# A decoder trunk with split fp32 weights: the low part of every fourth weight unit by an accumulating DMA

## The chip, the cores and the metric

The kernel runs on one core of one Trainium2 chip. The metric is device time in microseconds of one execution. Five engines work side by side, each with its own queue in program order: TensorE (PE, matmul; PEld is its weight load), VectorE (DVE), ScalarE (ACT), GpSimd (POOL) and SyncE (SP, which here only issues DMAs). They wait for each other by semaphores.

## The reference

Two layers of a hybrid decoder at 256 tokens and width 1024, all in float32. Each layer is a SwiGLU feed-forward block, a mixer and another feed-forward block, each behind an RMSNorm; the first layer's mixer is latent attention beside a gated MLP over chunks, the second's a short gated convolution.

```
def swiglu(h, w_gate, w_up, w_down):
    return (jax.nn.silu(h @ w_gate) * (h @ w_up)) @ w_down

for layer in range(DEPTH):
    x = x + 0.5 * swiglu(rms_norm(x, ffn_pre_norm[layer]), ...)
    h = rms_norm(x, mix_norm[layer])
    x = x + (mla_sgu_mixer if layer % 2 == 0 else short_conv_mixer)(h, ...)
    x = x + 0.5 * swiglu(rms_norm(x, ffn_post_norm[layer]), ...)
return rms_norm(x, final_norm)
```

With 256 tokens every weight is used once, so about 170 MB of weights pass through the core in one execution.

## The kernel before

TensorE multiplies in a rounded 32-bit format (fp32r). To stay near float32 each operand is split in two: a rounded part, hi, and what rounding lost, lo = x - hi. A product is then three matmuls: hi by hi, hi by lo and lo by hi (`mm_b`, L315 to L317: activation hi by weight hi, activation hi by weight lo, activation lo by weight hi; L316 is the one that reads the weight's low part).

The weights come in 162 units, numbered from 0, of mostly 128 x 2048 numbers (1 MB), in the order of the list `plan`: 22 units of gate and up weights and 11 of the down projection for each of the four feed-forward blocks (f0 to f3), 10 units and 4 of output projection for the attention mixer between f0 and f1, 12 and 4 for the convolution between f2 and f3. Each unit goes through four steps in `prefetch`: SP issues a load from HBM into `raw` (L136); ScalarE writes `whi`, the rounded copy, in two pieces of 1024 columns (L139, 320 of them); VectorE writes `wlo` = raw - whi in the same two pieces (L140); TensorE uses both in 24 matmuls of 512 columns (other counts in the mixers). Units 0 and 1 are cut differently (L130, L131).

`raw`, `whi` and `wlo` have three buffers each. `weights()` is called when a unit is about to be used and prefetches three units ahead (LOOKAHEAD), so what holds a unit back is its buffers: whi and wlo of unit n are those of unit n-3, and raw of unit n is free again when unit n-3 has been converted. In an output projection (`project_out`) the last two units (TAIL) are used together, column block by column block, so their buffers come back only at its end.

The order of instructions on each engine is set by a scheduler at build time, from the order of the program and priorities. Beside the units, ScalarE and VectorE work off the gate of the pair of units before (`gate`: SiLU L368, product L369, copies L376 and L377 of the transposed result, which TensorE makes in L374), and the norms (L269, L280, L281, L346). POOL does little: some constants, a mask (L520) and four copies in the attention mixer (L634).

Of the kernel before, what the change touches and what calls it, by code (L numbers as in the profile page):

```python
# [19 lines left out]
F32 = mybir.dt.float32  # L20
# [3 lines left out]
AF = mybir.ActivationFunctionType  # L24
ALU = mybir.AluOpType
# [41 lines left out]
def trunk(ctx: ExitStack, tc: tile.TileContext, io: dict, out: bass.AP, stop=None):  # L67
    nc = tc.nc
    V, A, G, PE = nc.vector, nc.scalar, nc.gpsimd, nc.tensor
# [39 lines left out]
    def prefetch(upto):  # L109
        while len(ready) < min(upto, len(plan)):  # L110
            src = plan[len(ready)]
            w = math.prod(src.shape[1:])
            raw = rawp.tile([P, WMAX], F32, name="raw")
            hi = hip.tile([P, WMAX], F32R, name="whi")
            lo = lop.tile([P, WMAX], F32R, name="wlo")
            n = len(ready)
            if n < 2:

                rv, hv, lv = (t.rearrange("p (f n) -> p f n", f=2) for t in (raw, hi, lo))
                cuts = ((0, 1), (1, 2), (2, 4)) if n == 0 else ((0, 2), (2, 4))  # L120
                for k0, k1 in cuts:
                    e = slice(k0 * 256, k1 * 256)
                    k, c, m = 4 * n + k0, 2 * n + k0 // 2, k0 % 2
                    nc.sync.dma_start(xt[c][:, m:m + k1 - k0, :], io["xT"][:, k:4 * n + k1, :])
                    nc.sync.dma_start(rv[:, :, e], src[:, :, e])
                for k0, k1 in cuts:
                    for k in range(4 * n + k0, 4 * n + k1):
                        split_to(mv[k], xt[k // 2][:, k % 2, :], col(C_PRE0 + k))
                    e = slice(k0 * 256, k1 * 256)
                    A.activation(hv[:, :, e], rv[:, :, e], AF.Copy)  # L130
                    V.tensor_tensor(lv[:, :, e], rv[:, :, e], hv[:, :, e].bitcast(F32), ALU.subtract)  # L131
            else:
                dst = raw[:, :w]
                if len(src.shape) == 3:
                    dst = dst.rearrange("p (a n) -> p a n", a=src.shape[1])
                nc.sync.dma_start(dst, src)  # L136
                for q in range(0, w, STEP):
                    e = slice(q, min(q + STEP, w))
                    A.activation(hi[:, e], raw[:, e], AF.Copy)  # L139
                    V.tensor_tensor(lo[:, e], raw[:, e], hi[:, e].bitcast(F32), ALU.subtract)  # L140
            ready.append((hi, lo))

    used = [0]
# [1 line left out]
    def weights():  # L145
        prefetch(used[0] + 1 + LOOKAHEAD)
        w = ready[used[0]]
        used[0] += 1
        return w
# [19 lines left out]
    def col(c):  # L169
        return small[:, c:c + 1]  # L170
# [17 lines left out]
    def split_to(m, src, scale=None):  # L188

        if scale is None:  # L190
            return (A.activation(m[:, :T], src, AF.Copy),
                    V.tensor_tensor(m[:, T:], src, m[:, :T].bitcast(F32), ALU.subtract))
        return (A.activation(m[:, :T], src, AF.Copy, scale=scale),
                V.scalar_tensor_tensor(m[:, T:], src, scale, m[:, :T].bitcast(F32), ALU.mult, ALU.subtract))
# [205 lines left out]

    norm = Norm(C_PRE0)
    prefetch(2)
    for b in range(2):
        for h in range(2):
# [28 lines left out]
    for j in range(KD):  # L433
        if j % 2 == 0:
            hi, lo = weights()
# [5 lines left out]
        hi, lo = weights()  # L441
# [29 lines left out]
    for h in range(2):  # L471
        for b in range(2):
            e = slice(b * 512, (b + 1) * 512)
# [333 lines left out]
```

## Time and profile before

| | |
|---|---|
| median of 2 timed runs | 962.16 us (961.34 to 962.99) |
| the profiled execution | 962.89 us, of which the profile's span is 961.2 us |
| busy: PE, DVE, ACT, POOL | 98%, 59%, 51%, 1% of the span |
| HBM read | 171.62 MB, 180 GB/s over the span |
| granted TensorE clock | 0.996 of full speed, mean |

The span is from the first to the last instruction; the execution's own time has 1.7 us around it. Busy matmul time is modelled from a pipeline, so consecutive matmuls overlap in the rows; an idle time on TensorE shows as a gap with the name of what ended it. The chain that ended last is followed back from the last instruction; what is off that chain had time to spare.

### The profile page before, as it was taken

What the parts mean: (1) busy time and instruction counts of PE and PEld (TensorE: products, weight loads), DVE (VectorE), ACT (ScalarE), POOL (GpSimd) and SP (SyncE); (2) the same over time, 40 slices, a digit from 0 to 9 for tenths busy, and PEclk for the clock granted to TensorE, in tenths of its full rate; (3) what the DMA queues carried; (4) which work ended last, traced back from release to release, by engine and by line L of the source; (5) the groups of instructions that cost most, each with busy time, mean ns of one, the idle gap of its engine ahead of it and who ended that gap; (6) DMA issues with size and microseconds to landing.
All of it is one profiled execution on the core that took longest, in us unless ns stands there. A gap on an engine that the chain in (4) does not pass through costs nothing.

```text
span 961.2 us, 11528 instructions
## 1 busy us (share of the span) xinstructions
PE 942.2 (98%) x4588; PEld 785.1 (82%) x4588; DVE 564.3 (59%) x800; ACT 486.4 (51%) x736; POOL 5.3 (1%) x13
## 2 busy tenths in 40 slices
PE   7999999999999999999999999999999999999996
PEld 5888888898978888888888888888888888888885
DVE  5765554477767555554475555544898765555433
ACT  7454444384757444443374444434655554454432
POOL 0000000001000000000000000000000000000000
PEclk9999999999999999999999999999999999999998
DMA  7865556545514655565556555564446465555541
GB/s 265 269 210 183 176 185 197 186 154 175 175 58 162 217 177 178 193 197 178 187 178 203 177 177 186 186 197 175 176 176 203 148 218 177 190 198 180 175 132 44
DMA packets 57446, 173.42 MB, mean 180 GB/s; under 512 B 2992, under 2 KB 3888, under 8 KB 54832
## 3 DMA queue, kind: packets, MB, share of 16 engines
q1 hardware_dynamic: 57392, 172.68, 53.1%
q8 instruction: 36, 0.59, 0.2%
q14 instruction: 18, 0.15, 0.0%
HBM read 171.62 MB, written 1.05 MB: 180 GB/s over the span
## 4 chain that ended last, share of the span: by engine, by line
PE 96%; DVE 1%; ACT 1%; DMA 1%; SPq 0%; issue 0%; DVEq 0%; ACTq 0%
PE ps L317 27%; PE ps L315 27%; PE ps L316 26%; PE ps L179 5%; PE ps L180 2%; PE psb L374 2%; PE ps L184 1%; PE ps L185 1%; PE ps L186 1%; PE psb L275 1%; DMA raw<-in_f_gu 1%; PE ps L587 0%; PE ps L589 0%; PE ps L588 0%; PE ps L655 0%; DVE wlo L140 0%
## 5 line engine op out<-in xcount | busy, mean ns | idle before, releaser
L140 DVE TENSOR_TENSOR wlo<-raw,whi 128x1024 fp32r<-128x1024 f32 x320 | 378.5, 1220 | 305.1 <-ACT whi L139 305.1
L139 ACT ACTIVATE whi<-raw 128x1024 fp32r<-128x1024 f32 x320 | 321.8, 1050 | 322.4 <-issue 167.4
L315 PE MATMUL ps<-whi,mv 128*128 128x512 f32 x704 | 279.2, 397 | 6.3 <-ACT whi L130 6.3
L316 PE MATMUL ps<-wlo,mv 128*128 128x512 f32 x704 | 275.6, 391 | 0.8 <-DVE wlo L131 0.8
L317 PE MATMUL ps<-whi,mv 128*128 128x512 f32 x704 | 275.4, 391 | 0.0
L315 PE MATMUL ps<-whi,a 128*128 128x512 f32 x416 | 163.4, 393 | 0.0
L316 PE MATMUL ps<-wlo,a 128*128 128x512 f32 x416 | 162.8, 391 | 0.0
L317 PE MATMUL ps<-whi,a 128*128 128x512 f32 x416 | 162.6, 391 | 0.0
L315 PEld LDWEIGHTS ps<-whi,mv 128*128 128x128 f32 x704 | 132.8, 189 | 33.4 <-ACT whi L130 7.2
L316 PEld LDWEIGHTS ps<-wlo,mv 128*128 128x128 f32 x704 | 132.9, 189 | 28.2 <-DVE wlo L131 2.0
L317 PEld LDWEIGHTS ps<-whi,mv 128*128 128x128 f32 x704 | 132.7, 188 | 28.0
L317 PEld LDWEIGHTS ps<-whi,a 128*128 128x128 f32 x416 | 78.1, 188 | 16.1 <-issue 0.2
L316 PEld LDWEIGHTS ps<-wlo,a 128*128 128x128 f32 x416 | 78.3, 188 | 15.6
L315 PEld LDWEIGHTS ps<-whi,a 128*128 128x128 f32 x416 | 78.1, 188 | 15.6
L368 ACT ACTIVATE silu<-ps,rn 128x256 f32<-128x256 f32 x88 | 41.3, 469 | 70.6 <-DVE silu L369 70.6
L179 PE MATMUL ps<-mv,whi 128*128 128x512 f32 x192 | 67.0, 395 | 0.0
L369 DVE SCALAR_TENSOR_TENSOR silu<-ps,rn,silu 128x256 f32<-128x256 f32 x88 | 42.2, 480 | 22.2 <-ACT silu L368 22.2
L180 PE MATMUL ps<-mv,wlo 128*128 128x256 f32 x192 | 53.1, 279 | 0.0
L179 PEld LDWEIGHTS ps<-mv,whi 128*128 128x128 f32 x192 | 35.9, 188 | 7.9
L281 DVE SCALAR_TENSOR_TENSOR mv<-psb,small,mv 128x128 fp32r<-128x128 f32 x80 | 26.6, 347 | 19.3 <-ACT mv L280 19.3
L180 PEld LDWEIGHTS ps<-mv,wlo 128*128 128x128 f32 x192 | 36.1, 188 | 0.6 <-DVE wlo L140 0.4
L377 DVE TENSOR_TENSOR a<-psb,a 128x512 fp32r<-128x512 f32 x44 | 30.2, 685 | 5.4 <-ACT a L376 5.4
(183 smaller groups left out, 584.2 us busy)
## 6 DMA issues: line engine op xcount, KB each, us to landing
raw<-in_f_gu SPq DMA_DIRECT2D x86, 1024.0 KB, 5.2
raw<-in_f_dn SPq DMA_DIRECT2D x44, 1024.0 KB, 5.2
raw<-in_c_cz SPq DMA_DIRECT2D x8, 1024.0 KB, 5.0
raw<-in_e_in SPq DMA_DIRECT2D x7, 1024.0 KB, 4.8
raw<-in_e_out SPq DMA_DIRECT2D x4, 1024.0 KB, 5.1
raw<-in_c_b SPq DMA_DIRECT2D x4, 1024.0 KB, 4.8
raw<-in_c_out SPq DMA_DIRECT2D x4, 1024.0 KB, 5.0
raw<-in_f_gu SPq DMA_DIRECT2D x3, 512.0 KB, 7.9
```

Source lines behind the costliest of these rows:

```text
L139: A.activation(hi[:, e], raw[:, e], AF.Copy)
L140: V.tensor_tensor(lo[:, e], raw[:, e], hi[:, e].bitcast(F32), ALU.subtract)
L179: PE.matmul(ps, lhsT=hi, rhs=m, start=first, stop=False)
L180: return PE.matmul(ps[:, :T], lhsT=lo, rhs=m[:, :T], start=False, stop=last)
L281: V.scalar_tensor_tensor(lo, src, g, hi.bitcast(F32), ALU.mult, ALU.subtract)
L315: PE.matmul(ps, lhsT=a[0], rhs=w[0], start=first, stop=False)
L316: PE.matmul(ps, lhsT=a[0], rhs=w[1], start=False, stop=False)
L317: PE.matmul(ps, lhsT=a[1], rhs=w[0], start=False, stop=last)
L368: A.activation(s[:, h], v[:, :, 0, :], AF.Silu, scale=rn[:, h:h + 1])
L369: V.scalar_tensor_tensor(s[:, h], v[:, :, 1, :], rn[:, h:h + 1], s[:, h], ALU.mult, ALU.mult)
L374: PE.transpose(pt[:, o:o + P], s[:, h, f, :], ident)
L377: V.tensor_tensor(lo, pt, hi.bitcast(F32), ALU.subtract)
```

## The change

In every fourth unit from the seventh on (n = 6, 10, ..., 158: 39 units, all of full size) VectorE's two subtractions are gone. ScalarE writes -hi into `wlo` from the rounded part, in two pieces, and then GpSimd issues one DMA for the whole unit that adds `raw` onto `wlo` in place: lo = -hi + raw. In these units TensorE waits for that DMA, and so does SP before it loads the next unit into the same `raw`. The other 123 units are as before.

```diff
                 nc.sync.dma_start(dst, src)
+                by_dma = n >= 4 and n % 4 == 2
                 for q in range(0, w, STEP):
                     e = slice(q, min(q + STEP, w))
                     A.activation(hi[:, e], raw[:, e], AF.Copy)
-                    V.tensor_tensor(lo[:, e], raw[:, e], hi[:, e].bitcast(F32), ALU.subtract)
+                    if by_dma:
+                        A.activation(lo[:, e], hi[:, e].bitcast(F32), AF.Copy, scale=-1.0)
+                    else:
+                        V.tensor_tensor(lo[:, e], raw[:, e], hi[:, e].bitcast(F32), ALU.subtract)
+                if by_dma:
+
+                    G.dma_start(out=lo[:, :w], in_=raw[:, :w], accum_op=ALU.add)
             ready.append((hi, lo))
```

In the changed kernel the lines behind stand 7 lower (L368 is L375, L376 is L383, L634 is L641). On ScalarE's queue the two new instructions stand behind the two roundings of their unit. This is the first of them, unit 6, in the first feed-forward block; before:

```order
L139 ACTIVATE whi<-raw 128x1024 x2
L376 ACTIVATE a_181<-psb 128x512
L368 ACTIVATE silu<-ps,rn 128x256 x2
L139 ACTIVATE whi<-raw 128x1024 x4
L376 ACTIVATE a_183<-psb 128x512
```

and in the changed kernel:

```order
L140 ACTIVATE whi<-raw 128x1024 x2
L142 ACTIVATE wlo<-whi 128x1024 x2
L383 ACTIVATE a_181<-psb 128x512
L375 ACTIVATE silu<-ps,rn 128x256 x2
L140 ACTIVATE whi<-raw 128x1024 x4
L383 ACTIVATE a_183<-psb 128x512
```

The two negations (L142) come ahead of the copy and the SiLU of the gate, which stand behind them.

On POOL's queue, from the first constants to the end, before:

```order
L161 AFFINE_SELECT ident<-ident 128x128
L516 AFFINE_SELECT mask<-mask 128x128
L520 AFFINE_SELECT wt<-wt 128x1024
L634 TENSOR_SCALAR kt_1751<-krot 64x512
L634 TENSOR_SCALAR kt_1752<-krot 64x512
L634 TENSOR_SCALAR kt_1753<-krot 64x512
L634 TENSOR_SCALAR kt_1754<-krot 64x512
```

and in the changed kernel:

```order
L168 AFFINE_SELECT ident<-ident 128x128
L523 AFFINE_SELECT mask<-mask 128x128
L147 DMA wlo<-raw 128x2048
L527 AFFINE_SELECT wt<-wt 128x1024
L147 DMA wlo<-raw 128x2048 x8
L641 TENSOR_SCALAR kt_1760<-krot 64x512
L641 TENSOR_SCALAR kt_1761<-krot 64x512
L641 TENSOR_SCALAR kt_1762<-krot 64x512
L641 TENSOR_SCALAR kt_1763<-krot 64x512
L147 DMA wlo<-raw 128x2048 x30
```

All 39 accumulating DMAs (L147) are issued here, nine of them (units 6 to 38) ahead of the four copies of the attention mixer and thirty behind.

## Rows read from the trace of the kernel before

**Rows 1.** The page: busy us, share of the span and instructions of each engine.
```profile
span 961.2 us, 11528 instructions
...
PE 942.2 (98%) x4588; PEld 785.1 (82%) x4588; DVE 564.3 (59%) x800; ACT 486.4 (51%) x736; POOL 5.3 (1%) x13
```
**Rows 2.** The page: the chain that ended last, shares of the span by engine.
```profile
PE 96%; DVE 1%; ACT 1%; DMA 1%; SPq 0%; issue 0%; DVEq 0%; ACTq 0%
```
**Rows 3.** Costliest groups: busy us, mean ns of one, idle before and its releaser.
```profile
L140 DVE TENSOR_TENSOR wlo<-raw,whi 128x1024 fp32r<-128x1024 f32 x320 | 378.5, 1220 | 305.1 <-ACT whi L139 305.1
L139 ACT ACTIVATE whi<-raw 128x1024 fp32r<-128x1024 f32 x320 | 321.8, 1050 | 322.4 <-issue 167.4
```
**Rows 4.** Waits, of the engines and of SP's queue: us in total, times, longest.
```profile
DVE wlo L140 <- ACT whi L139: 305.1, 140, 5.1
ACT whi L139 <- PE ps L317: 131.9, 67, 4.5
...
SPq L136 <- DVE wlo L140: 769.6, 142, 18.4
```
**Rows 5.** Timeline around unit 22: start us, us, engine, instruction, idle before it.
```profile
120.45 0.48 DVE L369 SCALAR_TENSOR_TENSOR silu<-ps,rn,silu 128x256 f32<-128x256 f32 x1 [0.54 <-ACT silu L368]
...
126.32 0.39 PE L317 MATMUL ps<-whi,mv 128*128 128x512 f32 x1
126.55 0.60 PE L374 MATMUL psb<-ident,silu 128*128 128x128 f32 x4
126.80 2.01 ACT L139 ACTIVATE whi<-raw 128x1024 fp32r<-128x1024 f32 x2 [3.43 <-issue]
127.89 2.36 DVE L140 TENSOR_TENSOR wlo<-raw,whi 128x1024 fp32r<-128x1024 f32 x2 [3.08 <-ACT whi L139]
124.84 5.81 SPq L136 DMA_DIRECT2D raw<-in_f_dn  x2
130.28 0.37 SPq L136 DMA_DIRECT2D raw<-in_f_dn  x1
...
138.25 0.48 PE L315 MATMUL ps<-whi,a 128*128 128x512 f32 x1
138.57 0.39 PE L316 MATMUL ps<-wlo,a 128*128 128x512 f32 x1
```
**Rows 6.** Timeline of units 26 and 66: start of the rounding, first matmul reading wlo.
```profile
150.10 1.06 ACT L139 ACTIVATE whi<-raw 128x1024 fp32r<-128x1024 f32 x1 [3.28 <-issue]
160.96 0.39 PE L316 MATMUL ps<-wlo,a 128*128 128x512 f32 x1
...
396.56 2.01 ACT L139 ACTIVATE whi<-raw 128x1024 fp32r<-128x1024 f32 x2 [0.94 <-PE ps L317]
407.88 0.39 PE L316 MATMUL ps<-wlo,mv 128*128 128x512 f32 x1
```
**Rows 7.** Timeline of units 34 and 130: start of the rounding, first matmul reading wlo.
```profile
199.36 1.05 ACT L139 ACTIVATE whi<-raw 128x1024 fp32r<-128x1024 f32 x1
206.76 0.28 PE L186 MATMUL ps<-mv,wlo 128*128 128x256 f32 x1
...
765.75 1.05 ACT L139 ACTIVATE whi<-raw 128x1024 fp32r<-128x1024 f32 x1
772.91 0.39 PE L316 MATMUL ps<-wlo,mv 128*128 128x512 f32 x1
```
**Rows 8.** The page: DMA queues (packets, MB, share of 16 engines), issues (KB, us to landing).
```profile
q1 hardware_dynamic: 57392, 172.68, 53.1%
...
raw<-in_f_gu SPq DMA_DIRECT2D x86, 1024.0 KB, 5.2
...
out<-o SPq DMA_DIRECT2D x4, 256.0 KB, 2.1
```
**Rows 9.** Timeline of POOL.
```profile
41.79 1.23 POOL L520 TENSOR_SCALAR_AFFINE_SELECT wt<-wt 128x1024 f32<-128x1024 f32 x1 [40.03 <-DMA wt<-in_sgw]
226.40 3.03 POOL L634 TENSOR_SCALAR kt<-krot 64x512 f32<-64x512 f32 x4 [183.39 <-ACT krot L632]
```
**Rows 10.** Stretches: us, busy time of each engine, granted clock, DMA share, GB/s.
```profile
0.00:5.00 5.00, 0.00 (x0) 0.00 (x0) 0.82 (x4) 2.35 (x4) 1.08 (x8) 1.00 0.49 148
12.00:20.00 8.00, 7.24 (x29) 5.81 (x29) 5.30 (x9) 8.00 (x19) 0.00 (x0) 0.79 0.92 345
240.00:290.00 50.00, 48.19 (x340) 40.99 (x339) 33.40 (x75) 33.00 (x72) 0.00 (x0) 1.00 0.36 125
```

## The prediction

> **What bounds the kernel now.** I read the busy shares first, then the chain, then the waits, and last the timeline of single weight units. TensorE is busy 98% of a span of 961.2 us [rows 1] and is 96% of the chain that ended last [rows 2]. VectorE (59%) and ScalarE (51%) are not the bound, and the 378.5 us of subtractions that the change thins out [rows 3] are off the path. So taking work from VectorE is worth next to nothing by itself: what can be won at all is the few per cent in which TensorE is not on the chain, and no large group of them is a wait for a low part. What can be lost is another matter. A weight unit has to be ready when TensorE comes to it, so the question is how much time a unit has and how much it needs.
>
> The waits [rows 4] show the clock of that supply. ScalarE's rounding L139 waits for TensorE's last product (67 times by L317): the rounded and the low parts have three buffers each, so unit n is converted only when TensorE is done with unit n-3. From there TensorE works for two units before it asks for unit n. I call this the window: from the start of the rounding of unit n to the first matmul that reads its low part (the second matmul of the unit). For unit 22, the first of the down projection, TensorE's last product of unit 19 starts at 126.32, the rounding starts at 126.80, and the first matmul that reads wlo starts at 138.57 [rows 5]: a window of 11.8 us. The subtraction of its second half ends at 130.25 (127.89 + 2.36), so 3.5 us of the window are used and 8.3 are spare.
>
> Reading the 39 changed units (6, 10, ..., 158) off the timeline like this gives: 11 windows of 11.8 us; 13 of 11.3 (unit 66: 396.56 to 407.88); 9 of 10.9 (unit 26: 150.10 to 160.96) [rows 6]; one of 13.3; and 5 short ones just behind the end of a stage (units 34, 50, 82, 114, 130: 7.4, 8.7, 9.3, 8.5, 7.2), because the last two units of an output projection are used together and give their buffers back late. The first and the last of these five are shown [rows 7].
>
> **The change, part by part.**
> - VectorE loses 78 subtractions of 1220 ns [rows 3], 95 us. Hidden before, worth nothing now.
> - ScalarE gets 78 instructions more (lo = -hi). The nearest row is the rounding itself, same size, same types out: two take 2.01 us [rows 5]. So 78 us in all, ScalarE rises from 486 to 565 us, still under 60%. What stands behind them on its queue is the copy of the products and the SiLU of the gate, 2 us later: in the pair before, VectorE's part of the SiLU ended at 120.93 (120.45 + 0.48) and TensorE transposed it at 126.55 [rows 5], 5.6 us of cover. If that cover went, it would be 2 us a unit.
> - The serial path of a changed unit becomes rounding 2.0 + negation 2.0 + the DMA, from the end of the negation until it has landed; call that D. Unlike the subtraction, which starts on the first half while ScalarE rounds the second, the DMA is one instruction for the whole unit and waits for all four activations.
> - D is not in this trace, so I bound it. A plain 1 MB load takes 5.2 us from issue to landing, and all loads together keep the 16 DMA engines 53.1% of the span busy for 172.68 MB, which is 3.1 us for a unit (0.531 x 961.2 x 1.049 / 172.68); the rest, 2.1 us, is fixed [rows 8]. From below: an add that costs no more than the shortest fixed part seen, 1.3 us (the 0.26 MB store, 2.1 less 0.8) plus one pass, 4.4. A gain of time is excluded there, since even that is longer than a subtraction. From above: four passes (two reads, a write, an add each at the load's rate), the fixed part and the slowest POOL instruction for writing out the transfer's list, 1.2 us [rows 9]: 2.1 + 12.4 + 1.2 = 15.7. I take two passes, because the engine has two megabytes to read (raw and lo) where a load has one, and half of POOL's 1.2: 5.2 + 3.1 + 0.6 = 8.9 us.
> - No other transfer is beside it: the load of unit 24 was issued at 124.84 and that of unit 25 at 130.28, when the subtraction of 22 gave raw back [rows 5]; the second now waits for the landing. That load is then late by about 9 us. Its rounding may start when TensorE is done with unit 22, that is 12.9 us of need and 5.4 of products (half of a 10.9 us window), about 18 us after 126.80; raw is given back 13 us after it and 5.2 us later the load is there. It just fits, and behind it stand the 8 us that an unchanged unit has to spare. SP's later loads queue behind this one and fit the same way.
> - On the SP queue one load moves behind two 256 KB ones early on, at most 1.6 us once; on POOL the four kt copies stand between two accumulations and are done at 229.4 (226.40 + 3.03) [rows 9], before unit 42 is converted. Both nothing.
>
> **The sum.** A changed unit needs 4.0 + 8.9 = 12.9 us. TensorE then waits 11 x 1.1 + 13 x 1.6 + 9 x 2.0 + 0 for the regular windows, 51 us, and 5.5 + 4.2 + 3.6 + 4.4 + 5.7 = 23 us behind the stage ends; 74 us together. One wait per four units does not shift the next, since its clock starts from TensorE. The profiled execution took 962.9 us (span 961.2); the two timed runs have a median of 962.2. Forecast: 962.2 + 74 = 1036 us.
>
> A rule on the price of an add: the Trainium skill, "Collectives: The Full Stack", section "The bandwidth ceiling: the fold count and why AG ≠ RS ≠ AR", says a reducing transfer runs at half a copy's rate, since it sends two reads through one read side and the add itself costs no cycles. No run here shows it; by it D has the two passes that I took. Another page speaks for the change: "DMA: Bandwidth & Descriptors", section "Anatomy of one DMA — SWDGE (gpsimd) path", gives a GpSimd DMA 2.0 us plus its bytes at 436 GB/s, an estimate of 6.8 us for two reads of 1.05 MB. By that the unit would need 10.8 us and the sum would be some 13 us, which is the first rival below.
>
> **Rivals.**
> - *The window covers it (not slower).* If D is 7.3 us or less the regular windows hold it but for 0.4 us in the nine short ones, and only the five units behind stage ends pay. At D = 5.2 (one pass): 1.8 + 0.5 + 0 + 0.7 + 2.0 = 5 us, 967 us. D = 7.3 is the point at which it decides: need 11.3, 9 x 0.4 + 15.4 = 19 us, 981 us. For it: 8 us are spare in every regular unit and the DMA engines are idle 47% of the time [rows 8], so they are free when the add comes. Against it: it needs an accumulating transfer, reading twice, to be no more than 2 us longer than a plain load. 20%.
> - *The add is much slower than two reads.* With three passes D = 2.1 + 9.3 + 1.2 = 12.6, need 16.6: 11 x 4.8 + 13 x 5.3 + 9 x 5.7 + 3.3 + 42 behind stage ends = 218 us, 1180 us. With four, need 19.7: 339 us, 1301 us. TensorE would then pause long enough to matter for its clock: after its only long pause, at the start, the granted clock was 0.79 over 12 to 20 us, part of it at the lower level (1.2 GHz), worth 1.7 us, while the short idle times of the middle (1.8 us in 50) left it at 1.00 [rows 10]. At 1.7 us for each of 39 waits that would be 66 us more. For it: nothing in this trace shows such a transfer, neither its add nor POOL's part. Against it: a read and a write can run side by side, as in a load. 32%.
> - *Faster.* Only if thinning VectorE removed a wait on the path; its share of the chain is 1% [rows 2]. 2%.
> - That the change does not do what it says: the subtractions are gone from VectorE's order and 39 DMAs stand on POOL's, so I give it nothing.
>
> **Numbers.** The forecast, D from 7.3 to about 10.7, has 46% and reaches from 981 to about 1108 us. Within 2% (943 to 981; about what can be told from no change) lies the covered case, and the edges: 20%; faster 2%; slower 78%. The range leaves out the slowest part of the second rival and almost nothing below: 967 to 1190 us.
>
> **What would show it.** In the profile after: POOL with 39 DMA issues, their median landing near 9 us (this number decides everything); TensorE's idle time mostly before L316, released by the DMA into wlo, some 39 times of 1 to 2 us and five of 4 to 6; VectorE down 95 us, ScalarE up 78; the granted clock still above 0.99. A landing under 7 us and no waits would prove the first rival right; over 11 us, or a clock that falls, the second. It would also be wrong if ScalarE's queue delays the SiLU so far that TensorE waits before its transposes.

## The result and the profile after

The changed kernel takes 1017.1 us (1015.97 to 1018.22, two runs), 1.057 times the 962.16 us of before, with a 95% interval of 1.051 to 1.063. The profiled execution took 1018.22 us, its span is 1016.5 us. It is 55 us slower. The forecast was 1036 us, slower, with a range of 967 to 1190.

The page of the changed kernel; the first two rows answer to [rows 1, 2], the queues and issues to [rows 8], the groups (busy us, mean ns of one, idle before and its releaser) to [rows 3]:

```profile
PE 961.9 (95%) x4588; PEld 791.3 (78%) x4588; DVE 475.1 (47%) x722; ACT 558.7 (55%) x814; POOL 38.7 (4%) x52
...
q1 hardware_dynamic: 57392, 172.68, 47.8%
q0 software_dynamic: 5616, 40.90, 20.8%
...
PE 72%; DMA 16%; ACT 7%; DVE 4%; issue 2%; SPq 0%; DVEq 0%; ACTq 0%; POOLq 0%
...
L323 PE MATMUL ps<-wlo,mv 128*128 128x512 f32 x704 | 281.2, 399 | 13.3 <-DMA wlo<-raw 11.2
...
L142 ACT ACTIVATE wlo<-whi 128x1024 fp32r<-128x1024 f32 x78 | 78.5, 1046 | 0.1
...
L147 POOL DMA_DIRECT2D wlo<-raw x39 | 33.2, 851 | 932.7 <-ACT wlo L142 800.5
...
raw<-in_f_gu SPq DMA_DIRECT2D x86, 1024.0 KB, 6.5
...
wlo<-raw POOLq DMA_DIRECT2D x39, 1024.0 KB, 7.2
```

VectorE fell by 89 us and ScalarE rose by 72, and neither engine is the bound. TensorE's share of the chain fell from 96% to 72%; the DMA has taken 16% of it. TensorE's idle time rose from 19.0 us (961.2 - 942.2) to 54.6, by 35.6 us, and its busy time by 19.7 us, though it does the same matmuls: together the 55.3 us of the span.

**A regular unit.** Unit 26, in the timeline of the changed kernel (start us, us, engine, instruction, idle before it), answers to [rows 6]:

```profile
152.57 2.01 ACT L140 ACTIVATE whi<-raw 128x1024 fp32r<-128x1024 f32 x2 [3.25 <-PE ps L324]
154.48 1.99 ACT L142 ACTIVATE wlo<-whi 128x1024 fp32r<-128x1024 f32 x2
...
156.77 0.85 POOL L147 DMA_DIRECT2D wlo<-raw  x1 [22.39 <-ACT wlo L142]
...
164.21 0.47 PE L323 MATMUL ps<-wlo,a 128*128 128x512 f32 x1 [0.62 <-DMA wlo<-raw]
```

Rounding and negation take 3.9 us. The DMA is issued 0.3 us later and lands some 7.3 us after that, so D is 7.6 us here (7.2 to 7.6 in 28 of the 32 regular units, 7.7 to 8.9 in units 6, 18, 118 and 122) and the need 11.5 us. The window was 10.9. TensorE waits 0.62 us.

**A stage end.** Unit 82, the third unit behind the output projection of f1:

```profile
513.16 1.07 ACT L140 ACTIVATE whi<-raw 128x1024 fp32r<-128x1024 f32 x1
514.26 1.28 ACT L258 ACT_TABLE_LOAD   x1
...
516.25 1.06 ACT L142 ACTIVATE wlo<-whi 128x1024 fp32r<-128x1024 f32 x1
...
517.32 1.28 ACT L264 ACT_TABLE_LOAD   x1
...
520.17 1.05 ACT L142 ACTIVATE wlo<-whi 128x1024 fp32r<-128x1024 f32 x1
...
521.51 0.85 POOL L147 DMA_DIRECT2D wlo<-raw  x1 [29.44 <-ACT wlo L142]
...
525.06 0.70 PE L322 MATMUL ps<-whi,mv 128*128 128x512 f32 x1 [2.40 <-ACT whi L140]
529.51 0.80 PE L323 MATMUL ps<-wlo,mv 128*128 128x512 f32 x1 [3.76 <-DMA wlo<-raw]
530.11 0.63 PE L324 MATMUL ps<-whi,mv 128*128 128x512 f32 x1
530.53 0.63 PE L322 MATMUL ps<-whi,mv 128*128 128x512 f32 x1
```

From the first rounding to the end of the second negation ScalarE takes 8.1 us (513.16 to 521.22), not 4: the norm's work, with two table loads of 1.28 us, stands between them. The landing comes 8.3 us later. The need is 16.3 us, and TensorE waits twice, 2.40 and 3.76 us (the first matmul there is one of unit 84, which the scheduler has put ahead of unit 82's low part). Then the matmuls start every 0.43 us in place of 0.23. The windows of the trace (length, busy us of PE, PEld, DVE, ACT and POOL, granted clock, DMA share, GB/s) show why, behind four of the stage ends:

```profile
218.00:221.40 3.40, 3.40 (x18) 3.40 (x17) 0.00 (x0) 0.00 (x0) 0.00 (x0) 0.50 0.98 368
334.00:340.80 6.80, 4.52 (x11) 3.60 (x12) 0.67 (x1) 0.00 (x0) 0.00 (x0) 0.50 0.84 299
525.20:535.40 10.20, 6.44 (x15) 4.70 (x16) 2.51 (x4) 0.65 (x2) 0.00 (x0) 0.50 0.98 281
818.70:828.90 10.20, 8.03 (x19) 5.84 (x19) 3.19 (x3) 1.36 (x2) 0.00 (x0) 0.50 0.98 283
```

The clock is granted at half, the 1.2 GHz level, for 3.4 to 10.2 us after or during such waits; in the middle of the kernel before it never was. TensorE is busy for 22.4 of these 30.6 us at half speed, which costs 11.2 us: more than half of the 19.7 us by which its busy time rose. The rest is for the most part the emptying and refilling of its pipeline at each wait, below.

The waits (us in total, times, longest), which answer to [rows 4]:

```profile
PE ps L323 <- DMA wlo<-raw: 18.6, 14, 4.5
...
PE ps L193 <- DMA wlo<-raw: 5.0, 2, 2.6
```

### The profile page after: what moved, and what is told of

Its sections match the earlier page's. It is cut to its first block, busy times and chain, and to the rows that moved or that the text cites. A ratio compares the mean times of both kernels' runs of the same rounds, so it can differ in the third digit from the quotient of the medians.

```text
span 1016.5 us, 11702 instructions
## 1 busy us (share of the span) xinstructions
PE 961.9 (95%) x4588; PEld 791.3 (78%) x4588; DVE 475.1 (47%) x722; ACT 558.7 (55%) x814; POOL 38.7 (4%) x52
## 3 DMA queue, kind: packets, MB, share of 16 engines
q0 software_dynamic: 5616, 40.90, 20.8%
## 4 chain that ended last, share of the span: by engine, by line
PE 72%; DMA 16%; ACT 7%; DVE 4%; issue 2%; SPq 0%; DVEq 0%; ACTq 0%; POOLq 0%
PE ps L323 21%; PE ps L324 20%; PE ps L322 20%; DMA wlo<-raw 14%; PE ps L186 3%; ACT whi L140 2%; PE psb L381 2%; PE ps L187 2%; ACT mv L287 1%; DMA raw<-in_f_gu 1%; ACT junk L276 1%; ACT wlo L142 1%; DVE wlo L144 1%; DVE x L353 1%; DVE mv L288 1%
## 5 line engine op out<-in xcount | busy, mean ns | idle before, releaser
L144 DVE TENSOR_TENSOR wlo<-raw,whi 128x1024 fp32r<-128x1024 f32 x242 | 285.6, 1219 | 348.3 <-ACT whi L140 347.9
L323 PE MATMUL ps<-wlo,mv 128*128 128x512 f32 x704 | 281.2, 399 | 13.3 <-DMA wlo<-raw 11.2
L322 PEld LDWEIGHTS ps<-whi,mv 128*128 128x128 f32 x704 | 134.6, 191 | 41.5 <-ACT whi L130 8.0
L324 PEld LDWEIGHTS ps<-whi,mv 128*128 128x128 f32 x704 | 134.8, 191 | 28.0
L323 PEld LDWEIGHTS ps<-wlo,a 128*128 128x128 f32 x416 | 78.2, 188 | 26.4 <-issue 10.9
L142 ACT ACTIVATE wlo<-whi 128x1024 fp32r<-128x1024 f32 x78 | 78.5, 1046 | 0.1
L375 ACT ACTIVATE silu<-ps,rn 128x256 f32<-128x256 f32 x88 | 41.3, 470 | 63.9 <-DVE silu L376 63.9
L147 POOL DMA_DIRECT2D wlo<-raw x39 | 33.2, 851 | 932.7 <-ACT wlo L142 800.5
L376 DVE SCALAR_TENSOR_TENSOR silu<-ps,rn,silu 128x256 f32<-128x256 f32 x88 | 42.2, 480 | 25.8 <-ACT silu L375 25.8
```

Of the source, the lines that this page charges most:

```text
L142: A.activation(lo[:, e], hi[:, e].bitcast(F32), AF.Copy, scale=-1.0)
L147: G.dma_start(out=lo[:, :w], in_=raw[:, :w], accum_op=ALU.add)
L322: PE.matmul(ps, lhsT=a[0], rhs=w[0], start=first, stop=False)
L323: PE.matmul(ps, lhsT=a[0], rhs=w[1], start=False, stop=False)
L324: PE.matmul(ps, lhsT=a[1], rhs=w[0], start=False, stop=last)
L375: A.activation(s[:, h], v[:, :, 0, :], AF.Silu, scale=rn[:, h:h + 1])
```

## The experiments

The theories, as the expectations name them. **A**: the loss is made at the stage ends, by a serial need that is longer than the window there, and the lower clock adds to it; regular units lose little. **P**: as I had predicted, every unit pays about the same by its need over its window. **C**: the accumulating DMAs slow the loads of the weights. **B**: ScalarE's negations delay the norms and the gate. All ratios are to the kernel before, run beside each on the same chip (962.2 to 963.1 us), each with its 95% interval.

**The regular units alone.** The accumulating DMA in all but seven units; those seven are subtracted on VectorE again.

```diff
-                by_dma = n >= 4 and n % 4 == 2
+                by_dma = n >= 4 and n % 4 == 2 and n not in (34, 42, 46, 50, 82, 114, 130)
```

> The accumulating DMA only in the 32 regular units; units 34, 42, 46, 50, 82, 114 and 130, at or behind the ends of stages, go back to the VectorE subtraction. Theory A (the loss is at the stage ends: waits of 1 to 6 us there, and the lower TensorE clock that follows them; the regular windows nearly cover the need of 11.5 us): the regular gaps seen in the changed kernel sum to 8 us, so about 970 us, clock above 0.99. Theory P (as predicted, every changed unit pays, 51 of 74 parts in the regular ones): about 1000 us. Theory C (the 41 MB more on the DMA engines slow the weight loads everywhere, 5.2 to 6.5 us to landing): 32 of 39 parts of the loss stay, about 1007 us. Theory B (ScalarE's negations delay the norms at the stage ends): as A, 965 to 970.

Measured: 976.8 us, 1.015 [1.013, 1.017].

```profile
PE 947.2 (97%) x4588; PEld 782.9 (80%) x4588; DVE 489.4 (50%) x736; ACT 546.0 (56%) x800; POOL 32.8 (3%) x45
...
raw<-in_f_gu SPq DMA_DIRECT2D x86, 1024.0 KB, 6.3
...
PE ps L323 <- DMA wlo<-raw: 7.0, 12, 1.3
```

The 32 regular units cost 14.6 us of the 55, 7 more than A had said; P is refuted. The clock did not fall in the middle. The 7 are found so: measured by the starts of matmuls around each first use of a low part, the 32 units take 15.0 us longer than before, of which 9.4 are waits that show as idle. The rest is 0.25 us at each of the 22 units that wait at all, most of them for less than 0.6 us: the last matmul before a wait runs out alone (0.39 us, where the next one otherwise starts after 0.23), and the second matmul behind it starts 0.31 us after the first, as in an empty pipeline; both count as busy time. C falls too: the loads take 6.3 us in place of 5.2, nearly as in the changed kernel, yet those 15.0 us are the whole loss, and the units without the DMA add nothing to it.

**The stage ends alone.** The same line turned around.

```diff
-                by_dma = n >= 4 and n % 4 == 2
+                by_dma = n in (34, 42, 46, 50, 82, 114, 130)
```

> The accumulating DMA only in units 34, 42, 46, 50, 82, 114 and 130; the other 32 changed units go back to the subtraction. Theory A: the loss less the 8 us of the regular gaps, about 1009 us, with the clock still falling to its lower level behind the stage ends (mean about 0.98). Theory P: 23 of 74 parts, about 979 us. Theory C: 7 of 39 parts, about 972 us.

Measured: 1003.4 us, 1.041 [1.038, 1.045].

```profile
PE 955.6 (95%) x4588; PEld 791.8 (79%) x4588; DVE 549.8 (55%) x786; ACT 499.5 (50%) x750; POOL 11.3 (1%) x20
...
raw<-in_f_gu SPq DMA_DIRECT2D x86, 1024.0 KB, 5.2
```

Seven DMAs cost 41.2 us, and 14.6 + 41.2 = 55.8: the two parts add up to the whole. TensorE's idle time rose by 26.2 us (1000.8 - 955.6 - 19.0) and its busy time by 13.4, with the clock at the lower level behind four of the seven. Loads are as fast as before here (5.2 us in the median), so a slowing of the weight loads is not what makes stage ends dear. The other way round it may be a part: D is 7.5 to 9.0 us at the seven places, up to 1.5 more than in a regular unit, and no run separates what transfers beside it cost there.

**Everything but the DMA.** The negation stays on ScalarE, and VectorE adds.

```diff
                         A.activation(lo[:, e], hi[:, e].bitcast(F32), AF.Copy, scale=-1.0)
+                        V.tensor_tensor(lo[:, e], raw[:, e], lo[:, e].bitcast(F32), ALU.add)
...
-                    G.dma_start(out=lo[:, :w], in_=raw[:, :w], accum_op=ALU.add)
```

> No DMA: in the same 39 units ScalarE writes -hi into lo as in the changed kernel, and VectorE adds raw onto it piece by piece (78 additions of 1.2 us). All of ScalarE's extra work stays, the need falls to about 5.3 us. Theories A, P and C (the DMA is what costs): 962 to 966 us. Theory B (ScalarE's 78 us in the norm and SiLU chains are a large part): 985 us or more.

Measured: 966.2 us, 1.0042 [1.0029, 1.0055]. ScalarE is as busy as in the changed kernel (558.9 us). So B is worth at most 4 us; the other 51 need the DMA.

**A DMA without the add.** The low part becomes a copy of raw, which leaves out the read of -hi and the addition; the place on every queue is the same.

```diff
-                    G.dma_start(out=lo[:, :w], in_=raw[:, :w], accum_op=ALU.add)
+                    G.dma_start(out=lo[:, :w], in_=raw[:, :w])
```

> The same DMA from POOL without the add: raw is copied over lo (so the low part is wrong; what is left out is the read of lo and the add). If the second read is what makes the DMA long, the median landing falls from 7.2 to about 5 us, the need to about 9.2, and the time to about 985 us (stage ends alone). If POOL's way of issuing or the SBUF to SBUF path sets it, the landing stays at about 7 us and the time at 1010 to 1017 us.

Measured: 977.2 us, 1.016 [1.014, 1.017].

```profile
q0 software_dynamic: 5616, 40.90, 10.8%
...
L147 POOL DMA_DIRECT2D wlo<-raw x39 | 20.9, 537 | 906.1 <-ACT wlo L142 777.9 <-ACT mv L287 60.1 <-DVE gain L435 29.0
...
wlo<-raw POOLq DMA_DIRECT2D x39, 1024.0 KB, 4.2
```

For the same packets and bytes the engines work 2.7 us a unit (0.108 x 977.6 / 39) in place of 5.4 (0.208 x 1016.5 / 39): the add doubles it. The landing falls by 3.0 us, 0.3 of it in POOL's issue (537 ns against 851). No regular unit waits; three stage ends still do (units 50, 82 and 130, by 1.1, 2.6 and 3.3 us), with the lower clock behind two of them. At unit 82 TensorE waits for the copy itself for only 0.2 us:

```profile
504.11 0.51 PE L322 MATMUL ps<-whi,mv 128*128 128x512 f32 x1 [2.40 <-ACT whi L140]
504.82 0.50 PE L323 MATMUL ps<-wlo,mv 128*128 128x512 f32 x1 [0.21 <-DMA wlo<-raw]
```

The 2.4 us are for the rounding of unit 84, whose first matmul stands ahead in TensorE's order and whose rounding stands behind the negations on ScalarE. Unit 130 is alike: its 3.3 us are all for the rounding and the subtraction of unit 131. So at these two places, in this order of TensorE's, a shorter DMA alone doesn't take the wait away.

**The DMA in two halves.** Each half is issued behind its own negation.

```diff
                         A.activation(lo[:, e], hi[:, e].bitcast(F32), AF.Copy, scale=-1.0)
+                        G.dma_start(out=lo[:, e], in_=raw[:, e], accum_op=ALU.add)
...
-                if by_dma:
-                    G.dma_start(out=lo[:, :w], in_=raw[:, :w], accum_op=ALU.add)
```

> The accumulating DMA is issued in two parts of 1024 columns, each behind the negation of its own half, so the first adds while ScalarE is still busy with the second half. Theory A (serial need against the window, with the clock on top at the stage ends): the need of a unit falls from about 11.5 us by some 1 us, to 10.3 to 10.7, since only the second half's transfer (about 2.7 us of the engines, behind the first half's) still lies behind the last negation; the regular waits (about 8 us in the changed kernel) go, and each stage end waits some 1 us less; the clock may fall as often. About 1000 us (995 to 1008). Rival F (a fixed cost per accumulating DMA, on POOL or in the queue, is what a unit pays): 78 issues in place of 39, the landing of the second half is not earlier than that of the whole was; 1017 us or more.

Measured: 985.7 us, 1.024 [1.022, 1.026], 9 us under the lower end of what A had said; rival F is refuted. The regular need is 10.4 us in most units, as expected. At a stage end the gain is larger, 2.0 to 5.0 us in six of the seven. Unit 82:

```profile
492.72 1.07 ACT L140 ACTIVATE whi<-raw 128x1024 fp32r<-128x1024 f32 x1
...
497.15 0.84 POOL L143 DMA_DIRECT2D wlo<-raw  x1 [24.76 <-ACT wlo L142]
...
501.08 0.85 POOL L143 DMA_DIRECT2D wlo<-raw  x1 [3.08 <-ACT wlo L142]
...
505.75 0.47 PE L321 MATMUL ps<-wlo,mv 128*128 128x512 f32 x1 [3.51 <-DMA wlo<-raw]
```

The norm's work lies between the two negations, so the first half (landed 502.0) is all but through when the second is issued at 501.08, and D is 4.8 us in place of 8.3 (negated 500.8, landed 505.6).

**The other phase.** Units 4, 8, ..., 160 (`n % 4 == 0`) in place of 6, 10, ..., 158.

> The same accumulating DMAs in the units 4, 8, ..., 160 (40 of them) in place of 6, 10, ..., 158. Of these only 48 and 116 have short windows before the change, 7.1 and 8.6 us. Theory A (the place decides: units behind a stage end pay 41 of the 55 us): 985 to 990 us, with waits at those two units, some at the odd regular one, and one or two falls of the clock. Theory P (each accumulating DMA costs its unit about the same, wherever it stands): 40 units of 1.4 us each, 1017 us.

Measured: 1023.6 us, 1.063 [1.061, 1.065]. My expectation failed by 34 us, and P's number was nearly met (7 us more). The waits say that its reason was not:

```profile
804.27 0.39 PE L322 MATMUL ps<-whi,a 128*128 128x512 f32 x1
808.65 0.77 PE L323 MATMUL ps<-wlo,a 128*128 128x512 f32 x1 [4.00 <-DMA wlo<-raw]
809.22 0.63 PE L324 MATMUL ps<-whi,a 128*128 128x512 f32 x1
```

This is unit 128, the last of an output projection. Its low part is asked for 8 us after its rounding (796.5) and comes 12 us after it. It is not used behind unit 127 but column block by column block together with it. I had counted it as following 127 and so taken its window for long. Units 32 and 112 are of the same kind (2.95 and 3.00 us), unit 4 stands at the start (4.10), and the units behind the stage ends wait too (48, 116, 132). The clock was at the lower level seven times ahead of the end, 41 us in all.

**The other phase without its stage ends.** 31 of the 40 units are left: nine, the named ones and their neighbours, go back to VectorE.

```diff
-                by_dma = n >= 4 and n % 4 == 0
+                by_dma = n >= 4 and n % 4 == 0 and n not in (4, 32, 36, 44, 48, 112, 116, 128, 132)
```

> The other phase (units 4, 8, ..., 160) gave 1023.6 us, where Theory A had said 985 to 990 and Theory P 1017. Its trace puts the waits not on the regular units but on 4 (start), on 32, 112 (one of the last two of an output projection, which are read together), and on 36, 48, 116, 132 and the units next to them; my reading of windows had missed these. Here the 31 units that are left: without 4, 32, 36, 44, 48, 112, 116, 128 and 132. Theory A (place decides): what remains are the waits seen at 28, 40, 72, 76, 108, 124, 156, 160, 4 us, their restarts and some small ones: 968 to 973 us, with no fall of the clock in the middle. Theory P (the price is paid by each accumulating DMA, 61 us over 40 units): 31 x 1.5 = 47, 1010 us.

Measured: 974.8 us, 1.012 [1.011, 1.014]; 2 us above A's range, 35 under P's number. So nine of the 40 units had made 49 of the 61 us, and no fall of the clock is left in the middle. It is the place that decides, and my list of the places was incomplete.

**The negation on VectorE.**

```diff
-                        A.activation(lo[:, e], hi[:, e].bitcast(F32), AF.Copy, scale=-1.0)
+                        V.tensor_scalar(lo[:, e], hi[:, e].bitcast(F32), -1.0, None, ALU.mult)
```

> As the changed kernel, but VectorE writes the negated rounded part (a multiplication by -1), half by half behind each rounding, in place of ScalarE; the accumulating DMA stays. Theory A (serial need, of which ScalarE's part is 4 us in a regular unit and 5 to 8 us behind a stage end, where its roundings and negations stand between the norm's work): the need falls by about 1 us in a regular unit and by 2 to 4 us behind a stage end; about 985 us (978 to 995). Rival D (the transfer alone decides behind a stage end, what comes before it is hidden): regular waits go, stage ends stay, about 1009 us. Rival V (VectorE's negation slows POOL's issue): the issue takes longer than 0.85 us and the unit gains nothing, 1017 us.

Measured: 988.4 us, 1.027 [1.025, 1.030].

```profile
L142 DVE TENSOR_SCALAR wlo<-whi 128x1024 fp32r<-128x1024 f32 x78 | 54.1, 694 | 81.5 <-ACT whi L140 81.4
L147 POOL DMA_DIRECT2D wlo<-raw x39 | 33.2, 852 | 909.5 <-DVE wlo L142 697.4
```

As A had it. The regular need is 10.2 us in most units, and no regular unit but the first waits. At unit 82 the negations are done 4.9 us after the first rounding in place of 8.1, and 3.5 us of wait are left of 6.2 (TensorE's order is another here too: unit 84's first matmul no longer stands ahead). POOL's issue is not slowed (852 ns), so rival V is out, and so is rival D: ScalarE's part of the need was worth 29 us.

**Both shortenings.** The halves and the negation on VectorE, in all 39 units.

```diff
-                        A.activation(lo[:, e], hi[:, e].bitcast(F32), AF.Copy, scale=-1.0)
+                        V.tensor_scalar(lo[:, e], hi[:, e].bitcast(F32), -1.0, None, ALU.mult)
+                        G.dma_start(out=lo[:, e], in_=raw[:, e], accum_op=ALU.add)
...
-                    G.dma_start(out=lo[:, :w], in_=raw[:, :w], accum_op=ALU.add)
```

> Both shortenings in all 39 units: the DMA in two halves and VectorE's negation. Alone they gave 985.7 and 988.4 us (before 963.0). Theory A: they shorten different pieces of the same serial path (the halves what lies behind the last negation, 4.8 us in place of 7.5 to 8.3; VectorE what lies ahead of it at a stage end, 4.7 to 4.9 us in place of 6 to 8), so the waits that either leaves (2 to 3.5 us at units 50, 82, 130) nearly go: 964 to 972 us. Rival (both remove the same time, or the stage ends wait for the first matmuls of the next unit whatever the low part does): 980 to 988 us.

Measured: 983.8 us, 1.022 [1.019, 1.024]. The two do not add, and I was wrong. The timeline of unit 82, and its windows:

```profile
491.12 1.07 ACT L140 ACTIVATE whi<-raw 128x1024 fp32r<-128x1024 f32 x1
...
492.96 12.88 SPq L136 DMA_DIRECT2D raw<-in_f_gu  x4
494.03 0.84 POOL L143 DMA_DIRECT2D wlo<-raw  x1 [24.41 <-DVE rn L246]
...
495.29 0.69 DVE L142 TENSOR_SCALAR wlo<-whi 128x1024 fp32r<-128x1024 f32 x1 [0.32 <-ACT whi L140]
496.28 0.85 POOL L143 DMA_DIRECT2D wlo<-raw  x1 [1.41 <-DVE wlo L142]
...
504.45 0.47 PE L321 MATMUL ps<-wlo,mv 128*128 128x512 f32 x1 [3.84 <-DMA wlo<-raw]
```

```profile
496.00:498.00 2.00, 2.00 (x11) 1.65 (x10) 0.35 (x1) 1.99 (x5) 0.85 (x1) 1.00 0.97 283
498.00:500.00 2.00, 2.00 (x11) 1.65 (x10) 1.99 (x3) 1.19 (x2) 0.00 (x0) 1.00 1.05 231
```

Counted from the unit's first rounding (491.12; 492.72 with ScalarE's negation), the second half is issued 3.2 us earlier (5.2 us behind it in place of 8.4) and yet lands 0.3 us later (13.2 in place of 12.9). In between all 16 DMA engines are busy: the load for the next unit but one, issued at 492.96 (the first of the four in that row), now runs beside the two halves, and each takes 8 us to land in place of 4.6 and 6.2 in a regular unit. That the two transfers shared the engines then is what the rows show; no run took that load away. The other places moved both ways: against the halves alone unit 50 waits 0.8 us in place of 2.4 and unit 130 2.8 in place of 4.8, but unit 114 3.1 in place of 1.9. In the regular units, where hardly a wait was left, the need falls further, to 9.2 us, and buys nothing. It is also more than four of the five short windows (7.2 to 8.7; the fifth is 9.3), which my expectation had overlooked.

**Halves, and none at the stage ends.** The halves of above with the seven units left out.

> Both mendings together: the accumulating DMA in two halves, and none in the seven units behind the stage ends (34, 42, 46, 50, 82, 114, 130, which VectorE subtracts as before). 32 units are left, with windows of 10.9 to 11.8 us and a need of about 10.5. Theory A: no wait for a low part is left, 963 to 968 us, no faster than before, since VectorE's subtractions lay beside TensorE's work. Rival F (a cost per accumulating DMA that the window does not hide): 977 us or more, as the version with whole-unit transfers and the same units.

Measured: 964.7 us, 1.0018 [1.0006, 1.0030].

```profile
PE 942.2 (98%) x4588; PEld 785.0 (82%) x4588; DVE 489.4 (51%) x736; ACT 545.9 (57%) x800; POOL 60.0 (6%) x77
...
PE ps L321 <- DMA wlo<-raw: 1.0, 1, 1.0
```

As A had it. TensorE is busy for the same 942.2 us as before, one low part is late by 1.0 us, and VectorE's 75 us fewer are worth nothing. This is the best version with the accumulating DMA, and none of them beats the kernel before.

## Why the prediction was right, and where it was not

- **Direction and cause: right.** The low part comes late because rounding, negation and one DMA stand in a row; the copy without an add and the halves shorten that row and give back 40 and 31 us. What VectorE loses is worth nothing, as the version at 964.7 us shows.
- **D: too large.** I took 8.9 us, two passes at a load's rate, the fixed part and half of POOL's slowest instruction. The engines' time was right in kind: 5.4 us, two times the plain copy's 2.7, if less than my 6.2. The Trainium skill, "Collectives: The Full Stack", section "The bandwidth ceiling: the fold count and why AG ≠ RS ≠ AR", has the reducing step of a collective at half a copy's rate; the two runs agree for this transfer, 20.8% and 10.8%. The fixed part was smaller than I took (some 2 us beside the 5.4, where I had 2.7), and D is 7.2 to 7.6 in most regular units. The Trainium skill, "DMA: Bandwidth & Descriptors", section "Anatomy of one DMA — SWDGE (gpsimd) path", gave the estimate of 6.8 us, which was nearer than mine (7.2 from issue; 4.2 for the plain copy, where the same estimate is 4.4).
- **The regular units: 51 us forecast, 14.6 measured.** With a need of 11.1 to 11.5 in place of 12.9 the windows of 11.8 us cover it and those of 11.3 all but do. The working was right and its first number was not, so almost the whole term went.
- **The stage ends: 23 us forecast, 41.2 measured.** Three things were wrong there. I used the need of a regular unit, 4.0 us for ScalarE, where the norm or the mixer's work stretches it to 5 to 8 us in six of the seven, and D is 7.4 to 9.9 there. ScalarE is also what makes unit 50's window short: its buffers, those of unit 47, were free at 306.1, but its rounding started only behind the norm's work, at 308.35; that the last two units of a projection are used together does not explain this one. I listed five units, and 42 and 46 wait as well (2.40 and 2.97 us; 46 is one of the two that are read together). And I kept the clock above 0.99 and gave its fall only to the second rival, as a matter of waits in every unit; it fell to 0.98 in the mean, behind four stage ends with waits of 2.6 to 6.2 us each, at a cost of 11.2 us.
- **So the forecast of 1036 us stood 19 us too high as the sum of two errors** of opposite sign. With the right D (7.4) my own formula would have given 984 us (6 us of regular waits and 16 behind five stage ends), close to the first rival at its point of decision, and would have missed by 33. The first rival's mechanism did happen, for the regular units; its price left out the same things at the stage ends.
- **What I had said would show it.** Landings near 9 us: 7.2. Some 39 waits of 1 to 2 us: the regular ones are of 0 to 1.1. Five of 4 to 6: seven places with 1.5 to 6.2. The loads queued behind on SP fit, as worked out: away from the stage ends the units without the DMA lose nothing (first experiment). The SiLU of the gate is not delayed to the point of a wait.

## What to carry to other kernels

A path that feeds the bound engine costs nothing until it is longer than its window, so list the windows from the rows that actually ask for the data, not from the order in the program: the ends of stages, and units that are read together, decide. Price the path at such a place with that place's own queue, not with a regular one. A wait of a few us on TensorE can cost more than itself: look at the granted clock behind it.

If a long transfer must stand in that path, cut it so that its first piece runs while the rest is being prepared; and ask which transfer it meets when it starts earlier.

## What the runs showed of the hardware

- A DMA that accumulates from SBUF to SBUF took twice the DMA engines' time of a plain copy of the same packets (5.4 against 2.7 us for a unit) and 3.0 us more to land (7.2 against 4.2). POOL needed 0.85 us to issue it, 0.54 for the plain one.
- Most waits of 1.9 us and more on TensorE were followed by 3.4 to 13.7 us at the 1.2 GHz level. The length of the wait alone did not tell: 1.91 us (unit 114, halves) and 2.12 us (unit 50, negation on VectorE) were followed by it, 2.40 and 2.97 us (units 42 and 46 of the changed kernel) were not. No wait of up to 1.8 us that stood by itself was.
- At each wait, however short, TensorE lost another 0.25 us that the profile counts as busy (22 waits of 0.03 to 1.3 us in the run of the regular units alone: 9.4 us idle, 15.0 lost).
- With one 1 MB load beside them two accumulating halves took 7.8 and 8.0 us to land, in place of 4.6 and 6.2 in a regular unit.
- VectorE wrote a negated copy of 128x1024 in 694 ns, ScalarE in 1046; the subtraction with two sources took 1219.
